# Preparing a mixing layer's parameters inside a feed-forward stage, and computing the delta units' rates in eight stages

## The chip, the core and the metric

The kernel runs on one core of one Trainium2 chip. A core has five engines that run side by side and wait for each other on semaphores: TensorE (PE, matmuls; its weight loads are PEld), VectorE (DVE), ScalarE (ACT), GpSimd (POOL) and SyncE (SP, which here only issues DMAs). Each engine works through its own queue in order. The metric is the device time of one execution in microseconds (us), as the median of several unprofiled runs.

## What is computed

Two decoder layers on x of 512 tokens x 1024 channels, float32. Cut to what matters here:

```python
for l in range(2):
    x = LN(a*x + 0.5*swiglu(x, ffn1_w_in[l], ffn1_w_out[l]))   # D_FF = 2816
    x = LN(a*x + mix(x))
    x = LN(a*x + 0.5*swiglu(x, ffn2_w_in[l], ffn2_w_out[l]))

def mix(x):                       # three causal token mixers on one projection h
    h = x @ w_in
    ya = rwkv7(h[..., :o1], rw_...)          # 8 heads of 64
    yb = diff_attention(h[..., o1:o2], ...)  # 4 heads
    yc = gated_deltanet(h[..., o2:o3], gd_conv_w, gd_a_log, gd_dt_bias, gd_norm_g)  # 4 heads
    merged = sum over n of sigmoid(gate_n) * (y_n @ w_branch[n])
    return merged @ w_out

# in gated_deltanet, the rates of the delta units, one per token and head:
g = -(exp(a_log) * softplus(a_lg + dt_bias))
beta = sigmoid(b_lg)
```

The small arrays of a layer's mix (rw_shift_mu, rw_w0, rw_w_up, ..., da_lam_*, gd_a_log, gd_dt_bias, the norm gains) are its parameters.

## The kernel before

Every large product is done in three fp32r matmuls on split operands (high x high, high x low, low x high; `mm3`). Weights come as `wr` tiles by DMA from SP, ACT casts the high part (`wh`), DVE subtracts to get the low part (`wl`). A projection of 128 columns is 24 matmuls on 512 columns, PSUM tile `pg`, `pu` or `pj`. Nearly every instruction goes through one helper, so the profile gives line 67 for all; they are told apart by their tiles.

A feed-forward stage (`ffn`) runs over groups of its 22 column blocks j, `GROUPS = [(0, 4), (4, 8), (8, 12), (12, 16), (16, 18), (18, 22)]`. Each j has two projections (pg, pu), then ACT's tanh and two DVE ops make `ft`, which is split. Behind the last j of a group its output product is added to acc (tiles `oa` in PSUM, evicted by DVE into `x`); the first four groups use a product with seven multiplications (`seven_acc`), with tiles `sa`, `sb`, `sr`, `sw`. `out_last` does the last group tile by tile, with the layer norm (`ln`, on DVE, ACT and POOL) and the transposes of the new x (`xtp`) between the matmuls, and begins the next stage's first three projections (`pe`).

`mix` runs `main` (lines 1478 to 1489): two projections, then twelve units in the order R D R D R R D G G D G G (R a pair of rwkv7 heads, D an attention head, G a delta head), then the gated merge. A unit projects its columns, and its head (`rw_pair`, `da_head`, `gdn_head`) is a Python generator that is put into the list `active`. Each `yield` of a head ends a stage. The order of issue is a planner's: `Estimate` keeps an estimated clock for each engine, and when `main` yields (after every two of the eight k-steps of a projection), `pump` issues the next stage of the first head in the list whose last stage has, by the estimate, ended before PE's clock, until PE's clock has gained 1300 ns. The tile framework then places the instructions on the engines' queues by the order of issue, by when their operands and buffers are free in a model of the run, and puts in the semaphores. Tiles of one tag share a pool of buffers and get them in the order of issue; a parameter tile has a tag and a buffer of its own, so that an instruction may be placed long before the place where it is issued.

The second unit is preceded by `gdn_ab` (line 1167), which projects the 8 columns of a_lg and b_lg and puts `gdn_scalars` (line 1181) into `active`. That generator yields once, at its start; then everything is one stage: four small transposes, a reduce, beta by a tanh, x = a_lg + dt_bias, softplus as max(x, 0) + log1p(exp(-|x|)) with a series of seven multiply-adds, g, and its split. These are 29 DVE ops on tiles of 128 x 16 (`ab`, `gb`, `gx`, `gy`, `gs`, `gq`, `gg`, `gh`, `gl`) in one dependent chain, and two ACT ops. The first `gdn_head` needs the result (`finish(3)`).

`params(l)` (lines 725 to 796) issues 20 DMAs from SP: eleven small vectors into `rows`, two into `lora`, `gup`, four into `lq`, `dtb` and `nea`. PE transposes rows (`prp`), DVE copies that to `pt` and derives `dv` in seven ops; lora and gup are split by ACT and DVE (three ops each); lq, ls and nea take five DVE ops and two of ACT. All readers are in `mix(l)`. It is called ahead of the first feed-forward stage of each layer (line 1550); for layer 0 that is behind `load_x` and `more_consts`, for layer 1 behind the second feed-forward stage of layer 0.

Of the kernel before, what the change touches and what calls it, by code (L numbers as in the profile page):

```python
# [20 lines left out]
DEPTH = 2  # L21
# [114 lines left out]
class Net:  # L136
# [23 lines left out]
    def sm(self, n, name, bufs=None):  # L160
        return self.smp.tile([128, n], F32, tag=name, name=name, bufs=bufs)
# [490 lines left out]
        product(P1, 1, 1, "T4", False)  # L652
        add(P1, 1, 0)

    def ffn(self, w_out, g, b, out=None):
        nc = self.nc
        acc = [[None, None] for _ in range(NT)]
        for g0, g1 in GROUPS:
            hs = []
            seven = g1 <= SEVEN  # L660
            for j in range(g0, g1):
                if j == NF - EWF:
                    self.early_w()
                pg = self.last(self.proj("pg"))
                if seven and j == g0 + 3:
                    next(rhs)
                pu = self.last(self.proj("pu"))
                if j == NF - 1:
                    self.wlast = self.last_w()
                t = self.t2(name="ft")  # L670
                nc.scalar.activation(out=t, in_=pg, func=ACTF.Tanh, scale=0.5)
                nc.vector.scalar_tensor_tensor(out=t, in0=t, scalar=1.0, in1=pg, op0=ALU.add, op1=ALU.mult)
                nc.vector.tensor_tensor(out=t, in0=t, in1=pu, op=ALU.mult)
                if not seven:
                    hs.append(self.split(t, "h"))
                elif j % 2 == 0:
                    hs.append(self.seven_lhs(t, None))
                    even = t
                else:
                    hs[-1] += self.seven_lhs(even, t)  # L680
                if seven and j == g0:
                    B = [self.seven_load(w_out, g0)]
                elif seven and j == g0 + 1:
                    B.append(self.seven_load(w_out, g0 + 2))
                elif seven and j == g0 + 2:
                    rhs = self.seven_rhs(B)
                    next(rhs)
            if seven:
                self.seven_acc(hs, rhs, 0.25 / ALPHA, acc)
            elif g1 < NF:  # L690
                self.out_acc(hs, 0.25 / ALPHA, acc)
        self.out_last(hs, 0.25 / ALPHA, acc, g, b, out)
# [488 lines left out]
    def gdn_scalars(self, ab):  # L1181
        nc = self.nc
        yield
        p2 = self.psum((128, 4, 16), "pab2")
        for tt in range(NT):
            self.tr(p2[:, tt, :], ab[:, 128 * tt:128 * tt + 128], self.ident[0:16, 0:16])
        p3 = self.sm(32, "ab").rearrange("p (t c) -> p t c", t=4)
        nc.vector.tensor_reduce(out=p3, in_=p2.rearrange("p t (g c) -> p t c g", g=2), axis=AX.X, op=ALU.add)
        p2 = p3
        sm = lambda n: self.prm.tile([128, 4, 4], F32, tag=n, name=n)  # L1190
        V = nc.vector
        x, y, s, q = sm("gx"), sm("gy"), sm("gs"), sm("gq")
        self.beta = sm("gb")
        nc.scalar.activation(out=self.beta, in_=p2[:, :, 4:8], func=ACTF.Tanh, scale=0.5)
        V.tensor_scalar(out=self.beta, in0=self.beta, scalar1=0.5, scalar2=0.5, op0=ALU.mult, op1=ALU.add)
        V.tensor_tensor(out=x, in0=p2[:, :, 0:4], in1=self.bc(self.dtb, 4), op=ALU.add)

        V.tensor_scalar(out=y, in0=x, scalar1=-1.0, scalar2=None, op0=ALU.mult)
        V.tensor_tensor(out=y, in0=x, in1=y, op=ALU.min)
        nc.scalar.activation(out=y, in_=y, func=ACTF.Exp)  # L1200
        V.tensor_scalar(out=s, in0=y, scalar1=2.0, scalar2=None, op0=ALU.add)
        V.reciprocal(out=s, in_=s)
        V.tensor_tensor(out=s, in0=s, in1=y, op=ALU.mult)
        V.tensor_tensor(out=y, in0=s, in1=s, op=ALU.mult)
        V.tensor_scalar(out=q, in0=y, scalar1=2.0 / 17, scalar2=2.0 / 15, op0=ALU.mult, op1=ALU.add)
        for n in (13, 11, 9, 7, 5, 3, 1):
            V.tensor_tensor(out=q, in0=q, in1=y, op=ALU.mult)
            V.tensor_scalar(out=q, in0=q, scalar1=2.0 / n, scalar2=None, op0=ALU.add)
        V.tensor_tensor(out=q, in0=q, in1=s, op=ALU.mult)
        V.scalar_tensor_tensor(out=q, in0=x, scalar=0.0, in1=q, op0=ALU.max, op1=ALU.add)  # L1210
        self.g = sm("gg")
        V.tensor_tensor(out=self.g, in0=q, in1=self.bc(self.nea, 4), op=ALU.mult)
        gh = self.prm.tile([128, 4, 4], F32R, tag="gh", name="gh")
        V.tensor_copy(out=gh, in_=self.g)
        gl = sm("gl")
        V.tensor_tensor(out=gl, in0=self.g, in1=gh.bitcast(F32), op=ALU.subtract)
        self.g2 = (gh.bitcast(F32), gl)
        self.eG = None
# [321 lines left out]
@with_exitstack  # L1540
def kernel(ctx: ExitStack, tc: tile.TileContext, a: dict, out: bass.AP):
    n = Net(ctx, tc, a)
    for l in range(DEPTH):
        n.plan_ffn(a["ffn1_w_in"][l], a["ffn1_w_out"][l])
        n.plan_mix(a["mix_w_in"][l], a["mix_w_branch"][l], a["mix_w_out"][l])
        n.plan_ffn(a["ffn2_w_in"][l], a["ffn2_w_out"][l])
    n.load_x(a["x"][0])
    n.more_consts()
    for l in range(DEPTH):
        n.params(l)  # L1550
        n.ffn(a["ffn1_w_out"][l], a["ln1_g"][l], a["ln1_b"][l])
        n.mix(l)
        n.ffn(a["ffn2_w_out"][l], a["ln3_g"][l], a["ln3_b"][l], out[0] if l == DEPTH - 1 else None)


# [23 lines left out]
```

## Time and profile before

| | us |
|---|---|
| median of 3 runs (2779.61 to 2780.69) | 2779.89 |
| the profiled execution | 2781.91 |
| its span, first to last instruction | 2780.2 |
| PE busy in the span | 2739.5 |
| DVE busy | 1929.4 |
| ACT busy | 1101.5 |
| POOL busy | 150.9 |
| mean granted TensorE clock, as a share of full speed | 0.997 |

In the span, the feed-forward stages lie at about 10 to 370, 1010 to 1400, 1400 to 1750 and 2400 to 2776 us, the two mixes between them. Times in the trace count from the start of the span. A matmul's end is modelled and matmuls overlap, so a busy PE isn't PE at its peak; a matmul at the lower clock counts as busy for longer. A wait for several semaphores is put down to the one that came last.

### The profile page before, as it was taken

Reading aid. Unit: us, or ns where it says so; the run is one execution under the profiler, and the core shown is the slowest. Engines: PE = TensorE matmul, PEld = TensorE weight load, DVE = VectorE, ACT = ScalarE, POOL = GpSimd, SP = SyncE. Lnnn points to the kernel's source line nnn. Section 1 sums busy time; section 2 is a strip of 40 time slices with the busy share of each in tenths; the row PEclk is TensorE's granted clock in tenths of the full one; section 3 lists DMA queues with packets and bytes.
Section 4 is the critical chain, followed back from the end, with each engine's and each line's share of the span. In section 5 each row is a group of like instructions: output and inputs, shape, how many; then the busy total and the mean of one; then the engine's idle time right before and its main releaser. Section 6 shows DMA issues by size and latency. Waiting matters only on the chain. (4 is left out here: it accounts for less than half of the span.)

```text
span 2780.2 us, 41956 instructions
## 1 busy us (share of the span) xinstructions
PE 2739.5 (99%) x16168; PEld 2262.4 (81%) x16168; DVE 1929.4 (69%) x4328; ACT 1101.5 (40%) x2005; POOL 150.9 (5%) x205
## 2 busy tenths in 40 slices
PE   9999999999999999999999999999999999999998
PEld 7888887778888888888888888877778878888887
DVE  6776567888785466667676665678787854666765
ACT  4333345444543333333333333455455433333332
POOL 1000021010000010000100000200000000100001
PEclk9999999999999999999999999999999999999999
DMA  6233422222232353332533324222222324533322
GB/s 208 91 107 106 140 79 71 60 65 69 71 81 81 96 178 114 118 103 84 149 110 111 109 92 139 84 68 58 68 66 68 88 80 121 174 114 99 115 75 84
DMA packets 437239, 277.56 MB, mean 100 GB/s; under 512 B 56952, under 2 KB 393008, under 8 KB 437040
## 3 DMA queue, kind: packets, MB, share of 16 engines
q1 hardware_dynamic: 437040, 274.89, 33.7%
q8 instruction: 127, 2.08, 0.3%
q14 instruction: 72, 0.59, 0.1%
HBM read 256.22 MB, written 18.63 MB: 99 GB/s over the span
## 5 line engine op out<-in xcount | busy, mean ns | idle before, releaser
L67 ACT CAST wh<-wr 128x1024 fp32r<-128x1024 f32 x342 | 360.0, 1053 | 763.7 <-issue 239.3
L67 DVE TENSOR_TENSOR wl<-wr,wh 128x1024 fp32r<-128x1024 f32 x342 | 421.5, 1232 | 317.7 <-ACT wh L67 315.8
L67 PE MATMUL pu<-xTh,wh 128*128 128x512 f32 x672 | 261.6, 389 | 0.4 <-DVE ft L67 0.4
L67 PE MATMUL pu<-xTl,wh 128*128 128x512 f32 x672 | 261.4, 389 | 0.0
L67 PE MATMUL pu<-xTh,wl 128*128 128x512 f32 x672 | 261.4, 389 | 0.0
L67 PE MATMUL pg<-xTh,wh 128*128 128x512 f32 x640 | 249.0, 389 | 0.0
L67 PE MATMUL pg<-xTl,wh 128*128 128x512 f32 x640 | 249.0, 389 | 0.0
L67 PE MATMUL pg<-xTh,wl 128*128 128x512 f32 x640 | 249.0, 389 | 0.0
L67 DVE SCALAR_TENSOR_TENSOR x<-oa,x 128x512 f32<-128x512 f32 x320 | 212.4, 685 | 36.1 <-PE oa L67 35.7
L67 PE MATMUL pj<-xTh,wh 128*128 128x512 f32 x560 | 228.1, 407 | 0.0
L67 PE MATMUL pj<-xTh,wl 128*128 128x512 f32 x560 | 222.7, 398 | 0.0
L67 PE MATMUL pj<-xTl,wh 128*128 128x512 f32 x560 | 222.4, 397 | 0.0
L67 DVE TENSOR_TENSOR ft<-ft,pu 128x512 f32<-128x512 f32 x84 | 57.7, 686 | 172.9 <-PE pu L67 172.7
L67 PE MATMUL pgt<-xTh,wh 128*128 128x512 f32 x384 | 154.1, 401 | 0.0
L67 PE MATMUL pgt<-xTl,wh 128*128 128x512 f32 x384 | 151.8, 395 | 0.0
L67 PE MATMUL pgt<-xTh,wl 128*128 128x512 f32 x384 | 151.0, 393 | 0.0
L67 PEld LDWEIGHTS pu<-xTh,wh 128*128 128x128 f32 x672 | 126.2, 188 | 26.7 <-DVE ft L67 0.7
L67 PEld LDWEIGHTS pu<-xTh,wl 128*128 128x128 f32 x672 | 126.1, 188 | 26.2
L67 PEld LDWEIGHTS pu<-xTl,wh 128*128 128x128 f32 x672 | 126.2, 188 | 26.0
L67 PEld LDWEIGHTS pg<-xTh,wl 128*128 128x128 f32 x640 | 120.1, 188 | 24.9
L67 PEld LDWEIGHTS pg<-xTl,wh 128*128 128x128 f32 x640 | 120.1, 188 | 24.9
L67 PEld LDWEIGHTS pg<-xTh,wh 128*128 128x128 f32 x640 | 120.1, 188 | 24.9
(420 smaller groups left out, 5897.2 us busy)
## 6 DMA issues: line engine op xcount, KB each, us to landing
wr<-in_ffn_w_in_dram SPq DMA_DIRECT2D x176, 512.0 KB
wr<-in_mix_w_in_dram SPq DMA_DIRECT2D x132, 512.0 KB
sw<-in_ffn_w_out_dram SPq DMA_DIRECT2D x128, 256.0 KB
wr<-in_ffn_w_out_dram SPq DMA_DIRECT2D x24, 512.0 KB
wr<-in_mix_w_branch_dram SPq DMA_DIRECT2D x24, 512.0 KB
xres<-x SPq DMA_DIRECT2D x40, 256.0 KB
x<-xres SPq DMA_DIRECT2D x40, 256.0 KB
wr<-in_mix_w_out_dram SPq DMA_DIRECT2D x16, 512.0 KB
```

The lines of the kernel that those rows point to most:

```text
L67: r = f(*args, **kw)
```

## The change

`params` is no longer called ahead of the first feed-forward stage of each layer. `ffn` gets an argument `then`, a layer whose parameters it issues ahead of j = 8, that is behind the second group's product: the first feed-forward stage of layer 0 does it for layer 0, the second one of layer 0 for layer 1. `gdn_scalars` gets seven more yields, so that its work is eight stages, with 3, 2, 5, 4, 4, 4, 4 and 3 DVE ops. The instructions themselves are the same.

```diff
--- before.py
+++ after.py
@@ -652,10 +652,12 @@
         product(P1, 1, 1, "T4", False)
         add(P1, 1, 0)
 
-    def ffn(self, w_out, g, b, out=None):
+    def ffn(self, w_out, g, b, out=None, then=None):
         nc = self.nc
         acc = [[None, None] for _ in range(NT)]
         for g0, g1 in GROUPS:
+            if g0 == 8 and then is not None:
+                self.params(then)
             hs = []
             seven = g1 <= SEVEN
             for j in range(g0, g1):
@@ -1194,20 +1196,25 @@
         nc.scalar.activation(out=self.beta, in_=p2[:, :, 4:8], func=ACTF.Tanh, scale=0.5)
         V.tensor_scalar(out=self.beta, in0=self.beta, scalar1=0.5, scalar2=0.5, op0=ALU.mult, op1=ALU.add)
         V.tensor_tensor(out=x, in0=p2[:, :, 0:4], in1=self.bc(self.dtb, 4), op=ALU.add)
+        yield
 
         V.tensor_scalar(out=y, in0=x, scalar1=-1.0, scalar2=None, op0=ALU.mult)
         V.tensor_tensor(out=y, in0=x, in1=y, op=ALU.min)
         nc.scalar.activation(out=y, in_=y, func=ACTF.Exp)
+        yield
         V.tensor_scalar(out=s, in0=y, scalar1=2.0, scalar2=None, op0=ALU.add)
         V.reciprocal(out=s, in_=s)
         V.tensor_tensor(out=s, in0=s, in1=y, op=ALU.mult)
         V.tensor_tensor(out=y, in0=s, in1=s, op=ALU.mult)
         V.tensor_scalar(out=q, in0=y, scalar1=2.0 / 17, scalar2=2.0 / 15, op0=ALU.mult, op1=ALU.add)
         for n in (13, 11, 9, 7, 5, 3, 1):
+            if n in (13, 9, 5, 1):
+                yield
             V.tensor_tensor(out=q, in0=q, in1=y, op=ALU.mult)
             V.tensor_scalar(out=q, in0=q, scalar1=2.0 / n, scalar2=None, op0=ALU.add)
         V.tensor_tensor(out=q, in0=q, in1=s, op=ALU.mult)
         V.scalar_tensor_tensor(out=q, in0=x, scalar=0.0, in1=q, op0=ALU.max, op1=ALU.add)
+        yield
         self.g = sm("gg")
         V.tensor_tensor(out=self.g, in0=q, in1=self.bc(self.nea, 4), op=ALU.mult)
         gh = self.prm.tile([128, 4, 4], F32R, tag="gh", name="gh")
@@ -1547,10 +1554,10 @@
     n.load_x(a["x"][0])
     n.more_consts()
     for l in range(DEPTH):
-        n.params(l)
-        n.ffn(a["ffn1_w_out"][l], a["ln1_g"][l], a["ln1_b"][l])
+        n.ffn(a["ffn1_w_out"][l], a["ln1_g"][l], a["ln1_b"][l], then=0 if l == 0 else None)
         n.mix(l)
-        n.ffn(a["ffn2_w_out"][l], a["ln3_g"][l], a["ln3_b"][l], out[0] if l == DEPTH - 1 else None)
+        n.ffn(a["ffn2_w_out"][l], a["ln3_g"][l], a["ln3_b"][l], out[0] if l == DEPTH - 1 else None,
+              l + 1 if l < DEPTH - 1 else None)
 
 
 # ---- launch: one core; inputs and outputs as the reference has them ----
```

## Rows read from the trace of the kernel before

**Rows 1.** The page, section 1: busy time, share of the span and instructions of each engine (whole run).

```profile
PE 2739.5 (99%) x16168; PEld 2262.4 (81%) x16168; DVE 1929.4 (69%) x4328; ACT 1101.5 (40%) x2005; POOL 150.9 (5%) x205
```

**Rows 2.** What PE waited for over the whole run: us in total, times, longest us.

```profile
PE pb L67 <- ACT sqh L67: 4.5, 2, 2.3
...
PE pw L67 <- DVE M L67: 1.7, 2, 0.9
...
PE pk L67 <- DVE gL L67: 0.4, 2, 0.2
```

**Rows 3.** Busy time of each engine around the two pb waits, in stretches of the span (us, then busy us and instructions of PE, PEld, DVE, ACT, POOL, the granted TensorE clock, DMA share, GB/s).

```profile
414.00:418.00 4.00, 4.00 (x19) 3.34 (x18) 3.73 (x11) 1.96 (x3) 1.28 (x3) 1.00 0.48 131
...
418.00:422.00 4.00, 1.66 (x23) 0.83 (x21) 3.44 (x12) 1.68 (x3) 0.00 (x0) 1.00 0.50 132
...
422.00:426.00 4.00, 4.00 (x23) 3.04 (x23) 1.88 (x5) 1.71 (x3) 1.28 (x1) 0.57 0.24 41
...
1800.00:1804.00 4.00, 1.69 (x23) 0.85 (x21) 3.59 (x12) 1.68 (x3) 0.00 (x0) 1.00 0.46 131
...
1804.00:1810.00 6.00, 6.00 (x35) 4.80 (x36) 2.74 (x5) 2.03 (x3) 1.28 (x1) 0.72 0.27 46
```

**Rows 4.** PE's instructions in order of time, layer 0 (start us, us, engine, line, operation; in brackets the idle time before it and what ended it).

```profile
420.74 0.50 PE L67 MATMUL pb<-sqh,r_bd 128*128 128x512 f32 x1 [2.27 <-ACT sqh L67]
```

**Rows 5.** ACT's instructions in order of time, layer 0, same columns.

```profile
414.83 1.18 ACT L67 CAST dk<-pj 64x512 fp32r<-64x512 f32 x2
...
418.99 1.18 ACT L67 CAST dk<-pj 64x512 fp32r<-64x512 f32 x2 [2.99 <-DVE dk L67]
...
420.07 0.62 ACT L67 CAST sqh<-sq 128x512 fp32r<-128x512 f32 x1
```

**Rows 6.** DVE's instructions in order of time, layer 0, same columns.

```profile
405.13 0.23 DVE L67 TENSOR_REDUCE ab<-pab 128x32 f32<-128x64 f32 x1
...
406.45 0.17 DVE L67 TENSOR_SCALAR n<-n 128x8 f32<-128x8 f32 x1
...
406.56 0.17 DVE L67 TENSOR_SCALAR gy<-gx 128x16 f32<-128x16 f32 x1
...
415.56 0.17 DVE L67 TENSOR_TENSOR gq<-gq,gy 128x16 f32<-128x16 f32 x1
...
415.77 0.17 DVE L67 TENSOR_SCALAR gq<-gq 128x16 f32<-128x16 f32 x1
...
416.93 1.23 DVE L67 TENSOR_TENSOR wl<-wr,wh 128x1024 fp32r<-128x1024 f32 x1
...
418.27 0.68 DVE L67 TENSOR_TENSOR dk<-pj,dk 64x512 fp32r<-64x512 f32 x1
...
420.12 0.17 DVE L67 TENSOR_TENSOR gl<-gg,gh 128x16 f32<-128x16 f32 x1
```

**Rows 7.** Busy time of each engine in other stretches, columns as in rows 3.

```profile
60.00:100.00 40.00, 38.93 (x170) 31.50 (x170) 25.94 (x39) 10.71 (x15) 0.00 (x0) 1.00 0.33 100
...
140.00:165.00 25.00, 25.00 (x112) 20.72 (x111) 11.01 (x14) 7.19 (x10) 0.00 (x0) 1.00 0.56 168
...
426.00:434.00 8.00, 8.00 (x48) 6.76 (x47) 4.18 (x18) 4.76 (x12) 0.00 (x0) 1.00 0.42 88
...
434.00:444.00 10.00, 10.00 (x52) 8.54 (x51) 9.58 (x40) 5.45 (x16) 0.00 (x0) 1.00 0.31 80
...
1165.00:1190.00 25.00, 25.00 (x112) 20.72 (x111) 11.07 (x13) 7.08 (x9) 0.00 (x0) 1.00 0.55 168
```

**Rows 8.** What PE waited for in five stretches: us in total, times, longest us. The first two rows are of 1380 to 1405 us (the boundary between the layers), the third of 2415 to 2440 (behind the second mix), the fourth of 60 to 100, the fifth of 1405 to 1460 and likewise of 2440 to 2480, the last of 28 to 40.

```profile
PE xtp L67 <- POOL x L67: 1.8, 3, 0.8
...
PE xtp L67 <- DVE x L67: 0.7, 1, 0.7
...
PE xtp L67 <- DVE x L67: 0.6, 1, 0.6
...
PE oa L67 <- DVE x L67: 1.0, 1, 1.0
...
PE oa L67 <- DVE x L67: 0.6, 1, 0.6
...
PE pu L67 <- DVE ft L67: 0.4, 1, 0.4
```

**Rows 9.** DVE's instructions in order of time at the boundary between the layers, columns as in rows 4: of the seven ops on lora, gup, lq and ls the first, the longest and the last.

```profile
1377.05 0.69 DVE L67 SCALAR_TENSOR_TENSOR lora<-lora 64x512 fp32r<-64x512 f32 x1
...
1380.28 1.72 DVE L67 SCALAR_TENSOR_TENSOR lora<-lora 64x512 fp32r<-64x512 f32 x1
...
1398.37 0.14 DVE L67 TENSOR_TENSOR ls<-ls 128x1 f32<-128x1 f32 x1
```

**Rows 10.** The instructions that write the tile rows, one for each layer (count: duration in ns min/median/max, start of the first and of the last in us): the memset and the first and the last of its eleven loads.

```profile
L67 POOL MEMSET rows<- x2: 210/212/213, 7.3 to 877.3; 128x128 f32 x2
...
L67 SPq DMA_DIRECT2D rows<-in_rw_shift_mu_dram x2: 485/1546/2606, 10.5 to 881.5; - x2
...
L67 SPq DMA_DIRECT2D rows<-in_da_norm_g_dram x2: 245/248/251, 26.0 to 896.1; - x2
```

**Rows 11.** SP's DMA issues in order of time, columns as in rows 4 (issues of one kind that follow each other are one row).

```profile
30.48 0.43 SPq L67 DMA_DIRECT2D nea<-in_gd_a_log_dram  x1
...
76.95 10.15 SPq L67 DMA_DIRECT2D wr<-in_ffn_w_in_dram  x4
```

## The prediction

> **What bounds the kernel now.** Read the page's head first [rows 1]: TensorE (PE) is busy for 2739.5 us, 99% of the span of 2780.2, so no more than 40.7 us of PE idleness is left. The change takes no matmul away. It can act only through the time in which PE waits and through stretches in which PE runs at the lower of its two clocks, so the second view is the list of what PE waited for [rows 2]. The longest kind in it is pb <- sqh: 4.5 us in two waits, one in each layer's mix. The third view is the stretch around these waits [rows 3]. In layer 0 PE is busy 1.66 of 4.00 us at 418 to 422, an idleness of 2.34 us; in the next 4 us it is busy throughout, but the granted clock is 0.57, a loss of 4.00 x 0.43 = 1.72 us. In layer 1 it is 4.00 - 1.69 = 2.31 us idle, and 6.00 x 0.28 = 1.68 us of clock. So **each stall costs about 4.0 us, 8.05 us in both layers**, and PE's busy share shows only half of it, for a slow matmul counts as busy.
>
> Why PE waits is read from the engines' orders in time. PE has been idle for 2.27 us when pb starts at 420.74, so it was free from 418.5 [rows 4]. ACT makes sqh at 420.07, at the end of its queue: two dk casts from 414.83 to 416.01, then nothing for 2.99 us until DVE has done a dk, two more casts at 418.99, then sqh [rows 5]. DVE, the engine that holds ACT, is full there (3.73 of 4.00 us at 414 to 418 [rows 3]). Among its work is the chain of `gdn_scalars`: the first op at 405.13, seven gq ops in a row from 415.56, a wl of 1.23 us at 416.93, only then the dk at 418.27; the last op of the chain at 420.12 [rows 6]. The chain is 29 DVE ops on 16 columns, mostly 0.17 us long. They start 0.21 us apart when they stand alone (415.56 to 415.77), and take only about 0.1 us of the queue when other work lies between (the next op starts at 406.56, 0.11 us after the one at 406.45) [rows 6].
>
> **Part 1: eight stages for the chain.** It adds and removes no instruction. Now all 29 ops are issued as one stage, ahead of every dq, dk, wl or sq op issued later; afterwards 3, 2, 5, 4, 4, 4, 4 and 3 are issued in turns of the planner. The first turn comes at the same place as now. A further one needs the planner's PE clock to pass the planner's end of the stage before, and the planner looks again after two k-steps of a projection, 6 matmuls, 6 x 25.00/112 = 1.34 us [rows 7]. Seven more turns take at least 9.4 us, so an even spread ends near 415 at the earliest, and later where DVE is behind by the planner's count. The whole chain is thus no longer than today's; what changes is that no more than a handful of its ops stand ahead of any one dk or sq. Without the run of gq ops the dk of 418.27 could start when its casts ended, at 416.0; the next two casts would take until about 417.3, sqh until 417.9, and PE, free at 418.5, would find it. One stage of four ops (4 x 0.21 = 0.8 us) in front of that dk gives a wait of 0.2, and with the wl of 1.23 us ahead as well, about 1.5. I take 0.9 per layer, between these and near the mix's next wait on DVE, pw at 1.7 us in two [rows 2]. A wait of that size leaves the clock alone: the 1.0 us wait of oa [rows 8] lies in 60 to 100 us, where the granted clock is 1.00 [rows 7]. **Gain 8.05 - 1.8 = 6.3 us; bounds 0 and 8.05.** That the chain ends later harms nobody directly: its reader is the first gdn_head, the eighth unit of twelve, while the chain starts in the second.
>
> Here a rule speaks against the change. The rows show the chain's ops at two prices, 0.21 and about 0.1 us of the queue [rows 6]. The Trainium skill, "VectorE: DVE Perf Modes", section "Rules for kernel authors", tells authors of chained ops to cut their count and not their semaphores, since the pipeline empties after each op in any case. By that rule 29 ops hold DVE for the same time however they are issued, part 1 would give nothing, and the time would be the first rival's. The trace agrees only in part, as its two prices differ by a factor of two.
>
> **Part 2: layer 1's parameters, out of the boundary between the layers.** Issued after the last feed-forward stage of layer 0, the loads of lora, gup and lq and seven DVE ops on them ran while the last layer norm of layer 0 was on its way: from 1377.05 to 1398.5, 0.69 us for the first, 1.72 for the longest, 3.9 together [rows 9]. The norms were late by as much, and PE waited 1.8 + 0.7 = 2.5 us for x; at the same place behind the second mix, where no parameters are prepared, it waited 0.6 [rows 8]. **Gain 1.9 us; bounds 1.5 (1.0 us left, as the largest wait of the kind elsewhere in rows 8) and 2.5.** The small vectors had been loaded at 877 to 896 already, as soon as their buffer was free [rows 10], and that stays so. The transpose prp and the eight ops on pt and dv move along.
>
> **Part 3: layer 0's parameters, out of the start.** There 20 DMAs stand in SP's queue, the small vectors from 10.5 to 26.0 us [rows 10] and the rest until 30.48 + 0.43 = 30.9 [rows 11]. ACT waits for lora ahead of an activation ft, and PE waits 0.4 us for that ft; the first x of the residual goes out late, and PE waits 1.0 us in oa where the other stages wait 0.6 [rows 8]. **Gain 0.4 + 0.4 = 0.8 us; bounds 0 and 1.0.**
>
> **Where both sets go.** Ahead of j = 8, behind the second product of a group: from about 140 us on, and 1165 for layer 1. DVE is busy 11.0 of 25 us in both stretches, ACT 7.2 and 7.1, PE 25.0 [rows 7]. One set takes 3.9 us of DVE [rows 9] and at most 9 x 0.21 = 1.9 for the ops on pt, dv and nea (an estimate by the chain's spacing [rows 6]), five ops of ACT, and one transpose that PE pays already. It fits more than twice over, so I cost it at **nothing**; without that cover, if the ops are pulled forward into the end of the group before, they delay an evict, and the waits of that kind are 0.6 to 1.0 us [rows 8], so 2 us for both layers at most. In SP's queue the 20 DMAs are set among the wr loads, of which four take 10.15 us to issue [rows 11]: those wait for free buffers, that is for PE, and lose nothing by a neighbour of 0.4 us.
>
> **Sum.** 6.3 + 1.9 + 0.8 = 9.0 us off the profiled execution of 2781.9 us (span 2780.2 and 1.7 around it): 2772.9. The median of the unprofiled runs is 2779.9, 2.0 below it, so the forecast is **2770.9 us**. One term has no place in the sum: the planner deals out the later stages of the mix anew. The mix's waits other than pb are 13 kinds, from pw (1.7 us) down to pk (0.4), some 15 us in both layers [rows 2]; a quarter of these either way is 4 us.
>
> **Rivals.** *The stall stays.* Eight turns at 1.34 us fill the same stretch, 405 to 418, with as many chain ops as today; sqh is late by 2 us and the clock falls. For it: DVE has 0.27 us free in 414 to 418 [rows 3]. Against: seven gq ops in a row before that dk can't come out of one turn any more. Then only parts 2 and 3 count, 2.7 us: 2777.2 us. Chance 0.24. *Slower.* The stall is moved and multiplied: chain stages fall into 434 to 444, where DVE is full (9.58 of 10.00 us [rows 7]) with the first da_head, and a matmul at the head of PE's order finds its operand 2 us late, with the clock loss behind it, as at pb. One such place costs 4.0 us per layer and 8.1 in all, if both layers show it as they both show pb. One place leaves 2779.0, no change; from two on it is slower: 2770.9 + 16.2 = 2787. Against: in between, at 426 to 434, DVE is half idle (4.18 of 8.00 us [rows 7]), which is room for 18 chain ops at 0.21. Chance 0.10 for two places, 0.05 for one. *The new deal helps.* The pb wait goes wholly and the mix's others shrink by a quarter: 2779.9 - 8.05 - 2.7 - 4 = 2765. Chance 0.08. *The preparation lands badly.* prp comes to PE before the last small vector of layer 0, and PE waits some 4 us with 2 to 4 of clock behind it: 2777 to 2779. Against: those loads depend on nothing but a memset at 7.3 us [rows 10], and SP has time for them before 140. Chance 0.03.
>
> **How the numbers follow.** The forecast has 0.50, the rivals 0.24, 0.10, 0.05, 0.08 and 0.03. About 0.2% (5.6 us) is what a measurement of this kernel can tell from no change: below 2774.3 is faster, above 2785.4 slower. Faster: the forecast, the good deal, and the part of the first rival in which half of the stall goes, 0.64. Same: the rest of that rival, one bad place, prp: 0.26. Slower: two bad places, 0.10. The range goes from the good deal, 2765, to the stall that stays with 3 us of bad deal, 2780. The forecast's own range, by the bounds of its parts, is 2767 to 2775.
>
> **What would show it.** Part 1 is right if the chain's ops stand in groups of at most five between other DVE work, pb waits under 1 us in each layer and the granted clock stays 1.00 behind it; wrong if pb waits 2 us again, or another row of 2 us stands in the list of PE's waits. Part 2: PE's waits for x at the boundary fall from 2.5 to about 0.6 us, and lora, gup and lq appear near 1165. Part 3: pu <- ft is gone from the list. The prediction fails if the mix's other waits change by more than 4 us, or if PE is no longer full near 140 or 1165.

## The result, and the profile after

The changed kernel took **2795.3 us** (median of 4 runs, 2795.0 to 2797.8) beside 2780.2 for the kernel before in the same measurement: a ratio of 1.0053, with an interval of [1.0041, 1.0064]. It is slower by 15 us, where 2770.9 was forecast and 2780 was the end of the range. In all, nine runs of it went from 2788.2 to 2797.8.

The page's first section shows the loss only in part: PE is busy for 7.3 us more than in [rows 1], in a span that is 13.1 us longer.

```profile
PE 2746.8 (98%) x16168; PEld 2267.7 (81%) x16168; DVE 1935.0 (69%) x4328; ACT 1099.6 (39%) x2005; POOL 158.7 (6%) x205
```

Every engine has as many instructions as before. So the question is again what PE waits for. The list of PE's waits over the whole run (us in total, times, longest us) corresponds to [rows 2]:

```profile
PE pS L67 <- DVE VU L67: 7.7, 2, 3.9
PE pb L67 <- DVE sql L67: 6.6, 6, 1.9
PE ip L67 <- DVE iZ L67: 3.6, 3, 1.8
PE pb L67 <- ACT sqh L67: 2.5, 4, 0.7
PE oa L67 <- DVE x L67: 2.4, 4, 0.6
PE xtp L67 <- DVE x L67: 1.7, 3, 0.6
```

The wait that the change was reckoned on, pb <- sqh, fell from 4.5 to 2.5 us, and above it stand three others, of which the longest single ones are 3.9, 1.9 and 1.8 us. All of them are in the mixes. The places are read from PE's instructions in order of time, layer 0 (start us, us, operation, idle time before it and what ended it):

```profile
411.67 0.49 PE L67 MATMUL pb<-sqh,r_bd 128*128 128x512 f32 x1 [0.57 <-ACT sqh L67]
...
413.90 0.49 PE L67 MATMUL pb<-sql,r_bd 128*128 128x512 f32 x1 [1.14 <-DVE sql L67]
...
478.88 0.50 PE L67 MATMUL pb<-sql,r_bd 128*128 128x512 f32 x1 [1.90 <-DVE sql L67]
...
576.62 0.80 PE L67 MATMUL pS<-VU,KB 128*128 128x128 f32 x2 [3.85 <-DVE VU L67]
...
857.59 0.68 PE L67 MATMUL ip<-iZ,imL 64*64 64x64 f32 x16 [1.77 <-DVE iZ L67]
```

The first pb now starts at 411.67, 9.1 us earlier than in [rows 4], and a second place of the same kind stands at 478.88, in the second rw_pair. Busy time in five stretches of the span (columns as in [rows 3]) shows what the waits cost, the clock among it:

```profile
412.00:418.00 6.00, 4.86 (x49) 3.76 (x49) 5.72 (x17) 1.91 (x3) 4.30 (x6) 1.00 0.44 104
...
474.00:486.00 12.00, 9.57 (x65) 6.98 (x63) 9.91 (x29) 3.84 (x6) 3.00 (x4) 0.86 0.29 66
572.00:577.00 5.00, 1.15 (x36) 0.96 (x34) 4.82 (x11) 3.67 (x7) 0.61 (x1) 0.89 0.01 3
577.00:586.00 9.00, 9.00 (x138) 6.79 (x139) 7.44 (x15) 2.61 (x6) 1.40 (x3) 0.68 0.28 69
...
858.00:864.00 6.00, 6.00 (x55) 4.44 (x51) 2.77 (x4) 2.16 (x4) 0.00 (x0) 0.72 0.00 0
```

At 572 to 577 PE works 1.15 of 5 us while DVE works 4.82. DVE's instructions in order of time say on what:

```profile
572.05 0.76 DVE L67 SCALAR_TENSOR_TENSOR be<-ta,AR 128x256 f32<-128x256 f32 x2 [0.51 <-ACT ta L67]
572.73 0.41 DVE L67 TENSOR_TENSOR AR<-AR,lw 128x252 f32<-128x252 f32 x1
573.06 0.75 DVE L67 SCALAR_TENSOR_TENSOR be<-be,G 128x448 f32<-128x448 f32 x2
573.73 0.41 DVE L67 TENSOR_TENSOR AR<-AR,lw 128x252 f32<-128x252 f32 x1
574.06 0.68 DVE L67 TENSOR_TENSOR sh<-sh,ta 128x512 f32<-128x512 f32 x1
574.77 0.68 DVE L67 SCALAR_TENSOR_TENSOR dq<-pj,dq 64x512 fp32r<-64x512 f32 x1
575.49 0.75 DVE L67 SCALAR_TENSOR_TENSOR sq<-sh,pt 128x512 f32<-128x512 f32 x1
576.27 0.29 DVE L67 TENSOR_TENSOR VU<-pU,R 64x128 f32<-64x128 f32 x1
```

An addition of 0.29 us (VU, a step of an earlier rw_pair's state loop) stands behind 4.2 us of other DVE work: the second stage of the fourth rw_pair and, within it, a dq. The matmul pS, at the head of PE's order, waits 3.85 us for it. No instruction of the chain stands in this burst: the chain's last one is at 422.97.

Part 2 did to PE's waits what was forecast: at the boundary xtp <- POOL x is gone, and 0.6 us of waiting for x is left, against [rows 8]. The two waits of part 3 are smaller as well: pu <- ft of the start is gone, and the 1.0 us of oa at 60 to 100 is 0.6. But that isn't the change's doing. Two of the runs below, E2 and E9, leave the parameters where they were, and they have no pu <- ft either and the same oa; this is all that PE waited for at 60 to 100 in E9:

```profile
PE oa L70 <- DVE x L70: 0.6, 1, 0.6
```

So the two waits are seen in the one profile of the kernel before, and in neither of the other two with the parameters in their old place. PE stays full where the parameters went, though DVE has 3.2 and 5.5 us more to do there than in [rows 7]:

```profile
140.00:165.00 25.00, 25.00 (x112) 20.71 (x111) 14.21 (x29) 7.17 (x10) 0.00 (x0) 1.00 0.53 159
1165.00:1190.00 25.00, 25.00 (x113) 20.63 (x112) 16.58 (x33) 8.85 (x12) 0.00 (x0) 1.00 0.49 148
```

To compare kernels I use two sums: **idle**, the span less PE's busy time (for the mixes, of 370 to 1010 and 1750 to 2400 us), and **clock loss**, each stretch of 2 us times one minus its granted clock, through the whole span. The expectations below give idle up to 0.9 us higher, since they count to the next whole microsecond. The sums can't simply be added: two profiles of the changed kernel have nearly the same idle, 46.5 and 46.7, and differ by 10.6 us in clock loss but by 6.8 in span (2793.3 and 2786.5), so by this one pair a microsecond of clock loss is worth some 0.64 of span. By that estimate the first of them lost 5.8 us to idle and some 8.5 to the clock against the kernel before, in a span 13.1 us longer. "Moved" compares the order in which the built programs list PE's matmuls: it counts the small ones, of 3022, that have another number of large ones (of projections, gates and output products) ahead of them; a place is one large matmul. (E7's expectation counts 2870 of them.)

| kernel | us | idle | of it mix 0, mix 1 | clock loss | small matmuls moved |
|---|---|---|---|---|---|
| before | 2780.2 | 40.7 | 10.3, 9.7 | 8.6 | - |
| changed | 2795.3 | 46.5 | 14.4, 14.4 | 21.9 | 2724 |
| changed, again | 2794.4 | 46.7 | 14.6, 14.5 | 11.3 | as changed |
| E1 parameters only | 2780.4 | 39.0 | 9.9, 10.4 | 12.1 | none |
| E2 eight stages only | 2790.1 | 48.1 | 14.4, 14.7 | 5.7 | as changed |
| E3 booked at once, spread | 2781.3 | 39.3 | 10.3, 10.4 | 10.5 | none |
| E4 not booked, at once | 2786.9 | 46.6 | 14.1, 14.5 | 7.7 | as changed but for 256 |
| E5 chain behind the stall | 2773.7 | 35.4 | 8.5, 8.4 | 6.5 | 436, by 3 to 8 places |
| E6 chain 40 us later still | 2777.1 | 35.7 | 9.1, 8.0 | 8.4 | 1600, by up to 6 |
| E7 booked twice | 2814.7 | 59.1 | 20.3, 21.7 | 31.7 | 2772 |
| E8 shorter burst | 2795.4 | 46.3 | 14.0, 14.6 | 21.9 | 954, from changed |
| E9 chain behind the stall alone | 2776.6 | 38.2 | 9.0, 8.7 | 4.1 | as E5 |

Idle and clock loss are of the one profiled run, the time is the median. In the first three rows 3.4, 17.1 and 6.8 us of the clock loss lie in the mixes; the rest is at the start and the end of the span. Beside the experiments the kernel before took 2781.0 (E1 to E4), 2781.9 (E5 to E7, the changed kernel again) and 2781.5 us (E8, E9, E5 again).

### The profile page after: what moved, and what is told of

It reads as the page before. It is cut to its first block, busy times and chain, and to the rows that moved or that the text cites. A ratio compares the mean times of both kernels' runs of the same rounds, so it can differ in the third digit from the quotient of the medians.

```text
span 2793.3 us, 41947 instructions
## 1 busy us (share of the span) xinstructions
PE 2746.8 (98%) x16168; PEld 2267.7 (81%) x16168; DVE 1935.0 (69%) x4328; ACT 1099.6 (39%) x2005; POOL 158.7 (6%) x205
```

## The experiments

**The two halves of the change.** E1 takes only the calls of `params` from the change, E2 only the seven yields.

> Only the move of params; gdn_scalars is one stage as before. PE's order of small matmuls in the mixes is then the one of before. Theory 1 (the move is worth what was forecast, and the loss comes from the planner dealing out the mix anew after the yields): 2777.2 us, 2.7 below before, with the pb waits of 2.2 us and their clock loss still there. Theory 2 (the moved preparation is what costs time): 2790 or more.

> Only the seven yields; params stays ahead of the feed-forward stage. PE's order of small matmuls in the mixes is the one of the changed kernel. Theory 1 (the new deal of the mix costs the time): about 2798 us, the changed kernel's 2795.3 plus the 2.7 that the move gives, with the waits of pS on VU (3.8 us), of pb on sql and of ip on iZ in both layers. Theory 2 (the moved preparation costs it): about 2772.

E1: 2780.4 us, ratio 0.9995 [0.9986, 1.0004]. E2: 2790.1, ratio 1.0035 [1.0021, 1.0049]. So the loss is that of the eight stages, though E2's time is 8 us below the 2798 expected; E1's lies above the 2777.2 of theory 1, which its interval just holds. PE's waits of E1, and then of E2:

```profile
PE pb L67 <- ACT sqh L67: 4.5, 2, 2.2
PE oa L67 <- DVE x L67: 2.3, 4, 0.6
```

```profile
PE pS L67 <- DVE VU L67: 7.7, 2, 3.9
PE pb L67 <- DVE sql L67: 6.6, 6, 1.9
PE ip L67 <- DVE iZ L67: 2.6, 4, 1.0
```

E1 keeps the old stall and loses the wait of xtp for POOL; its idle is 1.7 us lower than before. E2 has the new list.

**The stages have two effects, and they can be had one by one.** The chain is issued in pieces, and the planner's DVE clock is charged for it piece by piece, not for 29 instructions at once. In both runs here the chain's first three instructions are issued and charged as before. E3 charges the other 26 at once, as before, and issues them in seven parts, one a turn; E4 issues them at once and doesn't charge them. Both have the parameters moved.

```diff
+        if COUNTED:                      # True in E3, False in E4
+            for part in ops:
+                for eng, op, kw in part:
+                    self.est.log(eng, op, (), kw)
+        self.chain.extend(ops)
+        if not SPREAD:                   # True in E3: a part at each turn
+            self.drain()
```

> params moved; the chain is booked on the planner's clocks at once, as one stage like before, but its ops are issued in eight parts, one after each turn of the main generator. PE's order of small matmuls is exactly that of before, and only the place of the chain's 26 later ops on DVE and ACT differs. Theory 1 (the order that follows from the bookkeeping is what costs; spreading itself helps): 2769 to 2775 us, pb's first wait under 1.5 us and no drop of the clock behind it. Theory 3 (spread chain ops delay other DVE work by themselves): 2785 or more, with new waits beside gq ops.

> params moved; the chain's 26 later ops are issued in one go as before, but are not booked on the planner's clocks at all. PE's order of small matmuls is then that of the changed kernel but for 256 of 3022 that move by at most 6 places. Theory 1 (the order that follows from the bookkeeping costs the time, not the spread): 2790 to 2798 us with the waits of pS on VU and ip on iZ at the same places as in the changed kernel. Theory 3 (the spread itself costs): about 2777, as with params alone.

E3: 2781.3, ratio 1.0000 [0.9990, 1.0009]. E4: 2786.9, ratio 1.0023 [1.0014, 1.0032]. The charge alone deals the mix anew: E4's order on PE is the changed kernel's but for 256 small matmuls moved by at most 6 places, its idle is nearly the same, and its list has two of the new waits again:

```profile
PE pS L69 <- DVE VU L69: 7.7, 2, 3.9
PE pb L69 <- DVE sql L69: 6.3, 7, 1.9
```

Its time is below the 2790 expected, with less clock loss than the changed kernel. By the planner's code the way from the charge to the order is this: with the chain's 26 instructions not on DVE's clock, it takes DVE to be free earlier and issues the third stage of the first rw_pair sooner (pb 24 places earlier, in the changed kernel 26), and it deals all that follows from there.

E3 was a miss for the theory behind the forecast: no order on PE changed, the chain was spread over turns, and the stall stayed. DVE and then PE of E3 in order of time:

```profile
413.73 0.43 DVE L1241 TENSOR_TENSOR gs<-gs,gy 128x16 f32<-128x16 f32 x1
...
415.87 0.17 DVE L1241 TENSOR_TENSOR gq<-gq,gy 128x16 f32<-128x16 f32 x1
415.98 1.22 DVE L69 TENSOR_TENSOR wl<-wr,wh 128x1024 fp32r<-128x1024 f32 x1
...
417.32 0.68 DVE L69 TENSOR_TENSOR dk<-pj,dk 64x512 fp32r<-64x512 f32 x1
...
419.37 0.69 DVE L69 TENSOR_TENSOR dk<-pj,dk 64x512 fp32r<-64x512 f32 x1
```

```profile
419.79 0.50 PE L69 MATMUL pb<-sqh,r_bd 128*128 128x512 f32 x1 [2.50 <-ACT sqh L69]
```

The chain stands in a row as before, although it was issued in several turns: ten of its instructions from 413.73 to 415.98, then the wl, one more, the dk. The order of issue, by the numbers of the instructions in the built program, shows why. All seven parts were issued ahead of the first dk, and between them DVE was given no more than two dq and one wl, which the framework put ahead of the row. So the chain was spread over time, but not over DVE's other work. The order on DVE is not the order of issue either: that wl of 415.98 and both dk, issued behind the whole chain, stand ahead of its last instructions. The next runs therefore issue the chain later and tie it down as well; no run has the one without the other.

**Chain behind the stall.** E5 and E6 have the parameters moved and the chain charged at once, and tie the first DVE instruction of each of the seven parts behind the last one that DVE had been given by that turn; the parts begin 10 turns later (E5), or 30 (E6).

```diff
-        self.chain.extend(ops)
+        self.chain.extend([[]] * HOLD + ops)        # HOLD = 10 in E5, 30 in E6
...
+            pin = self.est.vector.last
...
+                    self.tc.add_manual_dep(ins, pin.name, mybir.DependencyInfo(
+                        mybir.DependencyClass.NoSync, mybir.DependencyReason.DATA), reason="pin")
```

> Parameters moved as in the change; the rates' chain is booked at once, as in the kernel before, so PE's small matmuls stand within 8 places of theirs, but its 29 instructions are tied in DVE's queue behind the third stage of the first rw_pair (the sq split and the two L products), so that none of them lies ahead of the sq split. Theory 1 (the wait of pb for sqh is the chain standing ahead of dk and the sq split in DVE's queue): pb<-sqh falls from 4.5-5.1 us over the run to under 1.5, no clock drop is left at 418-428, idle time falls by 3 us or more against the kernel with the parameters alone (39.4), time 2771-2777. Rival 1 (the wait is of the deal itself, wl and dk are late in any case): pb<-sqh stays above 3.5, time 2778-2783. Rival 2 (the chain is as costly where it is put): pb<-sqh falls, but waits on dsc, L or R behind the chain take its place, 2778-2782.

> The same, with the chain tied behind the work of some 20 turns later, around the second stage of the second rw_pair (some 50 us later). Theory 1: pb<-sqh under 1.5 us and no drop of the clock at 418-428, idle time 3 us or more under 39.4; what the chain costs at its new place is under 1 us a mix, since its results are first read some 170 us later: 2771-2777. Rival 2 (29 small DVE instructions stall PE wherever they stand while DVE is about 80% busy): a new wait of 2 us or more a mix near its new place, 2778-2783.

E5: 2773.7, ratio 0.9969 [0.9958, 0.9981]; E6: 2777.1, ratio 0.9983 [0.9974, 0.9992]. DVE, then ACT, then PE of E5 in order of time:

```profile
416.26 0.68 DVE L70 TENSOR_TENSOR dk<-pj,dk 64x512 fp32r<-64x512 f32 x1
...
421.47 0.16 DVE L1243 TENSOR_SCALAR gy<-gx 128x16 f32<-128x16 f32 x1
```

```profile
418.06 0.62 ACT L70 CAST sqh<-sq 128x512 fp32r<-128x512 f32 x1
```

```profile
418.73 0.49 PE L70 MATMUL pb<-sqh,r_bd 128*128 128x512 f32 x1
```

The dk stands at 416.26 (418.27 in [rows 6]), sqh at 418.06 (420.07 in [rows 5]), and pb starts at 418.73 without a wait, 2.0 us earlier than in [rows 4]. In neither mix of E5 does the granted clock fall, and PE's list has no pb <- sqh. That is theory 1: the chain in DVE's queue, ahead of dk, made the stall. In E6 the stall is gone as well, and idle is nearly as low, but it is 3.4 us slower than E5. PE waits 0.68 us for iZ at 462.80, as it does in E5 (0.81 at 464.69), and then 0.89 us for dmx at 464.33, which E5 doesn't have; a gy of the chain (0.87 us at 462.68) stands just ahead of that work in DVE's queue. The clock falls behind the two waits:

```profile
462.00:470.00 8.00, 6.43 (x48) 4.96 (x47) 7.68 (x27) 4.92 (x11) 3.05 (x5) 0.79 0.01 2
```

DVE is busy 7.68 of these 8 us. So 29 small instructions aren't free at any place, as rival 2 has it, though the new wait is under the 2 us given there and their price is below that of the old place.

**Another deal.** E7 charges the chain twice and issues it once; no engine gets another instruction.

```diff
-                for eng, op, kw in part:
+                for eng, op, kw in part * 2:
```

> Parameters moved; the chain is issued at once and once, as in the kernel before, but the planner's DVE clock is charged for it twice. No instruction is added or removed on any engine; only the order is dealt anew (2654 of 2870 small matmuls move, by -60 to +51 places). Theory 2 (any other deal than the one in the kernel before costs some 4 to 5 us of idle PE time per mix, since that deal was one that happens to fit): idle in the mixes 14 us each, 2786-2795. Rival (the deals scatter to both sides; the one that the eight stages make is just an unlucky one): idle in the mixes 9-12 us each, 2776-2784.

> The changed kernel once more, on the same chip and in the same rounds as the others. Theory: idle time as before (47, 14.4 in each mix), since the order of instructions is fixed; the time lost to the clock may differ from the 22 us of the first profile. If that loss belongs to this order of work, granted clock 0.991-0.992 and 2793-2797; if it belongs to the chip or the run, 0.993-0.998 and 2784-2791.

E7: **2814.7**, ratio 1.0119 [1.0106, 1.0133], worse than any range given. Its longest waits:

```profile
PE pj L69 <- DVE dq L69: 10.1, 2, 5.1
PE pb L69 <- ACT sqh L69: 7.3, 6, 2.3
```

A third deal with a third list, and its longest waits are on DVE's queue, or on ACT behind it. Both new deals are worse than the old one; whether others would be better, two can't show. The changed kernel again: 2794.4, ratio 1.0044 [1.0031, 1.0057]; its profiled run was the fastest of five, at 2788.2 and a mean granted clock of 0.996, the other four had 0.992 to 0.994. The idle is that of the order of work, then; the clock loss varies from run to run with the same order.

**The burst.** E8 is the changed kernel without the instructions at 574.06 and 575.49 and their like in layer 1, of the fourth rw_pair alone, whose keys and bonus term get other values by it:

```diff
-        TT(out=k, in0=k, in1=ta, op=ALU.mult)
-        STT(out=sq, in0=r, scalar=P["r_k"](j), in1=k, op0=ALU.mult, op1=ALU.mult)
+        if j == 3:      # charged to the planner, not issued
+            V = self.nc.vector
+            self.est.log(V, "tensor_tensor", (), dict(out=k, in0=k, in1=ta))
+            self.est.log(V, "scalar_tensor_tensor", (), dict(out=sq, in0=r, in1=k))
+        else:           # the two as before
...
```

> The changed kernel, with two of the seven DVE instructions of the burst of 572-576 us left out (the product of k with its rate, 0.68 us, and that of r, r_k and k, 0.75 us; of the fourth rw_pair alone, in both layers), while the planner's clock is still charged for them. What is left out changes the values of that pair's keys and of its bonus term. Theory (the 3.85 us that the state matmul pS waits are the burst that stands ahead of a 0.29 us addition in DVE's queue): the wait of pS for VU falls by the 1.43 us left out, from 3.85 to about 2.4 per layer, idle falls by some 3 us over the run. Rival (pS waits for something else that ends just then, and the burst only fills the time): the wait stays at 3.5-3.9.

2795.4 us, ratio 1.0053 [1.0037, 1.0069], no gain: idle is 46.3, not 3 us lower as expected. PE's waits of E8 in 569 to 580:

```profile
PE pj L67 <- DVE dq L67: 1.8, 1, 1.8
PE pS L67 <- DVE VU L67: 1.7, 1, 1.7
```

The wait for VU fell by 2.1 us: the two left out (1.43), and a dq (0.69) that now stands behind VU and not ahead of it. So the wait is for VU's place in DVE's queue. But 1.8 of the 2.1 came back in the next matmul that needs DVE, the pj that waits for that dq. With the 1.43 us out, that dq starts only 0.63 us earlier (575.97, not 576.60), for an iZ op of 0.85 us now stands ahead of it. What PE waits for here is DVE's queue as a whole and not the place of one addition in it. (Some matmuls behind this place moved too, by 1 to 16 places.)

**Only the chain.** E9 ties the chain as in E5 and leaves the parameters where they were; E5 was run beside it.

> The kernel before with its parameters where they were, and only the chain tied behind the third stage of the first rw_pair. If the parts add up: pb<-sqh under 0.5 us as in the run with both; the boundary and the start idle as in the kernel before (3.1 and 5.5); idle 38-39 against 36.1 with both; time 2774-2777, that is some 2 us over the run with both. Rival (the gain of the run with both needs the parameters out of the way): 2779-2782.

> The run with both (parameters moved, chain tied behind the third stage) once more, on another day's chip beside its part: the same order of work, so idle 36 again; clock loss 4-9; 2771-2776. If the first run was lucky with the clock only: 2777-2781.

E9: 2776.6, ratio 0.9982 [0.9974, 0.9991]; E5 again: 2773.8, ratio 0.9973 [0.9963, 0.9983]. PE's waits at the boundary between the layers (1365 to 1420 us), in E9 and in E5 again:

```profile
PE xtp L70 <- POOL x L70: 1.8, 3, 0.8
PE xtp L70 <- DVE x L70: 0.7, 1, 0.7
```

```profile
PE xtp L70 <- DVE x L70: 0.5, 1, 0.5
```

So the chain behind the stall gives 4.9 us, the parameters 2.8 more, and E5 is faster than both kernels of the case: some 8 us under the one before, some 21 under the changed one.

## Why the prediction was wrong

**The step that failed** is the sentence at the end of the sum: "One term has no place in the sum: the planner deals out the later stages of the mix anew", with "a quarter of these either way is 4 us". It was the largest term of all. The mixes' idle went from 20.0 to 28.8 us, and their clock loss from 3.4 to 17.1 (6.8 in the second profile). E4, which has the new deal without the turns, shows nearly the same idle in them, 28.5; E3, which has the turns without the new deal, has 20.8. The bound took the waits of the old deal and let them scatter. But those are what was left over with stages and DVE's work dealt in a certain way; another deal brings waits of other kinds, pS <- VU at 3.9 us where the old list has nothing over 2.3. E7 shows how far this goes: 42.1 us of idle in the mixes.

**Part 1** also failed in its own mechanism. "Without the run of gq ops the dk of 418.27 could start when its casts ended" is right, as E5 shows, but "no more than a handful of its ops stand ahead of any one dk" is not: eight stages don't take the run away. In E3 ten instructions of the chain still stand in a row, and pb waits 2.5 and 2.6 us in the two layers. This is the rival "the stall stays", for the reason given there: the turns fill the same stretch ahead of the dk. What was set against it, that seven gq ops in a row "can't come out of one turn any more", is true and doesn't help, since several turns follow each other with nothing else issued for DVE. In the changed kernel too the chain stands in rows of seven and six, against the sign of at most five; the first of them on DVE, layer 0:

```profile
419.76 0.15 DVE L67 TENSOR_TENSOR gq<-gq,gy 128x16 f32<-128x16 f32 x1
...
420.99 0.17 DVE L67 TENSOR_TENSOR gq<-gq,gy 128x16 f32<-128x16 f32 x1
421.20 0.70 DVE L67 TENSOR_TENSOR dk<-pj,dk 64x512 fp32r<-64x512 f32 x1
```

These rows hold up no pb, for in the new deal the sq split comes ahead of them (its sql stands at 413.17). The first pb's waits did fall there, to 0.57 + 1.14 us in layer 0, about twice the 0.9 that I took, since the third stage was issued earlier and not since the chain was spread: E4, with the chain in one go, has 1.02 + 0.90.

The **price of the stall** was too high as well: 8.05 us for both layers, against 4.9 measured when it is taken out alone (E9). In the profiles the idle of the mixes falls by 2.3 us, where the two waits were 4.5: about half of the wait comes back at other matmuls. The mixes' clock loss falls by the 3.4 us reckoned, 1.7 in each layer, but at the 0.64 estimated above that is worth 2.2 us, and 2.3 + 2.2 is near the 4.9 measured.

**"A wait of that size leaves the clock alone"** doesn't hold as said. In one profile the wait of 1.14 us at 413.90 leaves the granted clock at 1.00, and its twin in layer 1, 1.13 us at 1800.38, has a clock of 0.72 at 1800 to 1806.

**Part 2** was right: 1.9 us forecast, and PE's idle at the boundary (1380 to 1420 us) is 2.5 us in the kernel before, E2 and E9 and 0.7 to 0.8 in every profile with the parameters moved. **Part 3** was not: no run shows its 0.8 us, for the two waits that it was taken from are gone in E2 and E9 too, with the parameters in their old place. They were read from a single profile. That 2.8 us were measured between E9 and E5 again, beside the 2.7 forecast for both parts, is thus in part luck: the boundary explains 1.7 of them. E1's interval, 3.9 us of gain to 1.1 of loss, holds the 2.7 and the 1.9 alike.

In the changed kernel even part 2 doesn't show in the time: by the ratios that kernel is slower than E2 by 2 to 5 us (the intervals overlap), though its idle is 1.6 lower and its order on PE in the mixes the same. The granted clock was 0.991 to 0.996 in its runs, 0.993 to 0.998 in E2's and 0.994 to 0.997 in E4's, which has the parameters moved and nearly the same order. The wait for iZ at 857 is 1.7 or 1.8 us in three profiles with both halves of the change (E8's is one) and 0.9 in E2's. What brings that about is open.

The forecast's **own range** doesn't follow from its parts: their bounds give 2768.4 to 2778.4, not 2767 to 2775.

**The rival "slower"** (0.10, 2787) named the mechanism: a matmul at the head of PE's order finds its operand late behind a full DVE, with the clock loss behind it, in both layers. Its places and its cause were wrong. It put chain stages at 434 to 444; the waits are at 479, 572 and 857, with the chain over at 423. Its counter-argument, room on DVE at 426 to 434, was about the chain and so about nothing that decided.

**The rule of the Trainium skill**, "VectorE: DVE Perf Modes", section "Rules for kernel authors" (cut the count of chained ops), stood well in E3: as many instructions in other turns gave nothing (2781.3 us beside 2781.0). It isn't the whole: E5 has the same 29 and gains, since what counts beside their number is which instruction stands behind them in the queue.

## What to carry to other kernels

Where a planner deals the work out by its own estimate, a change of what it is charged for is a change of the whole order behind it. Compare the order of the built programs first, and if thousands of matmuls move, expect other waits, not the old ones scaled. To take a stall away, move the instructions that cause it and leave the books as they are: here the chain held back behind the stall gave 5 us, and the eight stages cost 9 to 15. See in the trace that a spread is a spread: work issued over several turns still stands in a row where nothing else is issued for that engine between them, and the order of issue need not be the order on the engine. And before a wait goes into a sum, look whether a second profile with the same code in that place has it too.

## What the runs showed of the hardware

The same program with nearly the same idle loses different amounts to the clock. Two profiles of the changed kernel, the same stretches, first and second run:

```profile
1866.00:1874.00 8.00, 7.25 (x28) 5.56 (x29) 5.29 (x20) 1.11 (x2) 1.28 (x1) 0.57 0.43 99
```

```profile
858.00:864.00 6.00, 6.00 (x75) 4.26 (x74) 3.40 (x6) 2.42 (x6) 0.00 (x0) 1.00 0.11 35
...
1866.00:1874.00 8.00, 7.73 (x44) 6.12 (x43) 5.71 (x25) 3.68 (x8) 1.28 (x1) 1.00 0.53 107
```

At 858 to 864 the first had 0.72, at 1866 to 1874 0.57, the second 1.00 in both; over the run 21.9 and 11.3 us. In pieces, the losses behind single waits were mostly near 1.7 or 3.4 us (1.72 in [rows 3], 8.00 x 0.43 = 3.44 in the first row here). What decides between them, these runs don't show.
